# Held weight sums and a new order of the seven products in a two-layer hybrid decoder trunk

## The chip, the cores and the metric

One core of one Trainium2 chip runs the whole program. The metric is the device time of one execution in microseconds (us). The core has a matrix engine (PE, TensorE), three engines for elementwise work (DVE, ACT for ScalarE, POOL for GpSimd), a queue of transfers that SP issues and another that POOL issues, whose transfers can add to what stands at their destination.

## The reference

A trunk of two layers on 1024 tokens of width 1024, in float32. Layer 0 mixes tokens with a causal convolution module, layer 1 with a causal mean over several windows; behind each comes a SwiGLU feed-forward block of width 2816; one RMSNorm ends the trunk.

```python
for i in range(DEPTH):
    sh_m, sc_m, g_m, sh_f, sc_f, g_f = jnp.split(c_act @ ada_w[i] + ada_b[i], 6, axis=-1)
    h = modulate(rms_norm(x, norm_mix_g[i]), sh_m, sc_m)
    y = conformer_conv(h, ...) if i % 2 == 0 else multiscale_pool(h, ...)
    x = x + (1.0 + g_m)[:, None, :] * y
    h = modulate(rms_norm(x, norm_ffn_g[i]), sh_f, sc_f)
    y = (silu(h @ w_gate) * (h @ w_up)) @ w_down
    x = x + (1.0 + g_f)[:, None, :] * y
return rms_norm(x, final_g)
```

What the change touches is the last `@ w_down` of layer 1, its addition to x, and the last `rms_norm`.

## The kernel before

The activations lie with channels on the 128 partitions and tokens along the free axis; the tokens are two chunks of 512, A and B, and x is eight tiles of 128 x 512 per chunk. Float32 products are made of three matmuls each: an operand is split into a rounded high part (ScalarE's copy) and a low part (DVE's subtraction), and high x high, high x low and low x high are added up in a bank. A matmul has 512 columns, or 256 in the last piece. A loaded weight block is split the same way into a tile `w` (line 126 issues every operation of DVE, ScalarE and POOL, line 148 every matmul, lines 158 and 165 transfers of SP's and POOL's queue).

Layer 1 uses fewer products than a plain multiplication: its gate and up products come as "joints", and its down product as seven products of a 2 x 2 block scheme (Winograd's form of Strassen's). The down weights are four blocks A11, A12, A21, A22 per group q (`wds[q, 0..3]`, q = 0 to 5; a group is 128 x 1024, the last one half of it). The other side is two kinds of sums of the activations over both chunks, which the joints write to DRAM (`kinds_d`, `kept_d`; `paired` at 1237 to 1250 makes them) and which are loaded again as operands. The weights of the products are A12 (p2), A11 (p1), S2 = S1 - A11 (p6), S3 = A22 - S2 (p7), A22 (p4), S1 = A21 + A22 (p5) and S4 = A12 - S2 (p3).

`weights_of` (1426 to 1458) loads the weights of a group and splits them, `operand` (1460 to 1476) does so for the other side. For S1 and S2, SP loads one block and POOL's queue adds the other into the same tile (1438, 1440). A11 goes into a held block `s2` in a slot of the tag h0; later DVE turns it into S2, and at p3 into S4. Other blocks take one of five raw tiles. The halves of the operands take slots of h1. h0 and h1 have eight slots each, a tile waits for the last reader of the slot, and products read h0 and h1 up to the end of the joints. Per group these are eight transfers: A11, two for S1, two for S2, one each for S3, S4 and A22.

`Seven` (1482 to 1532) runs the products: a step is one group of one product, its loads are issued four steps ahead (`LOADED`) and its splits two steps ahead (`SPLIT`). A full step is 24 matmuls: two operand tiles, four banks, three each. The banks come from a pool of six; when a product is done, DVE adds the four banks to the tiles of x they belong to (`update`), which frees them. The order before:

- p2 for q 4 and 5 (its first four groups run earlier, by `one_half`), p1, p6, p7, p4, p5, then p3 for q 0, 1, 5 in p5's banks, and last p3 for q 2, 3, 4 by halves of 256 columns (`ending`).
- `final(A)`, the last norm of chunk A, begins after p4: squares, their sum over the partitions by TensorE (`var`), a root by a short chain on DVE (`col`, `var`), a spread of it over the partitions (`rstd`), then DVE multiplies each of eight tiles and SP writes it out.
- `ending` does the same for B by halves of 256 tokens, so that the first half (B1) is multiplied while the second (B2) is still summed.

The order of TensorE's work is the order of the code. A scheduler orders the other engines and the transfers by its own estimates; `order(...)` gives an instruction an edge "behind the products", so that it isn't put ahead of what TensorE does at that point of the code. In `weights_of` only POOL's adds have this edge; SP's loads haven't.

Of the kernel before, what the change touches and what calls it, by code (L numbers as in the profile page):

```python
# [16 lines left out]
P = 128  # L17
# [114 lines left out]
def trunk(ctx, tc, xT, c, vec, ada, adan, w1f, w1, wdg, w2, wgu, wdn, wds, wpl, out):  # L132
# [1043 lines left out]
    def joint(l, fp, between=None):  # L1176
        c = {}

        def part(name, banks, after, again, before=None):
            def emit(take):  # L1180
                if before is not None:
                    before()
                if not again:
                    c[banks] = two_banks(banks)
                wt, h = take(), st["T"][name]
                todo = [(o, j) for o in range(2) for j in range(4)]
                if fp == 0 and name != "n4":
                    todo.sort(key=lambda oj: oj[1])
                for o, j in todo:
                    b = c[banks][o]  # L1190
                    products(b, wt, 4 * o + j, h[j], j == 0 and not again, j == 3, more=True)
                    if j == 3:
                        after(o, b)
                        pace()
            return emit

        def load():
            c["r1"] = [tmp.tile([P, TMPW], F32, tag=tag, name=nm("r1"), bufs=2) for tag in ("acc", "ny")]
            for o, r in enumerate(c["r1"]):
                sync.dma_start(r, rd[l][fp][:, o])  # L1200

        def after6(o, b):
            c["r2", o] = r = window(512, "r2")
            V_.tensor_tensor(r, c["r1"][o], b, op=SUB)

        def after5(o, b):
            if fp:
                r = temp(512)
            else:
                c["r15"] = c["r15"] if o else block("u0", "r15", F32)  # L1210
                r = c["r15"][:, o]
            c["r15", o] = r
            V_.tensor_tensor(r, b, c["r1"][o], op=ADD)
            if STRASSEN[l] and o:
                st["taken"] = V_.last.ins.name

        def ended(r, i, f, op):
            def after(o, b):
                t = c["r1"][o] if r == "r1" else c[r, o]
                V_.tensor_tensor(t, b, t, op=op)  # L1220
                c["c", o] = t
                if fp == 0 and r == "r15" and o:
                    st["read"] = V_.last.ins.name
                    for ins in st["next"]:
                        tc.add_manual_dep(ins, st["read"], edge, reason="behind the first unit's reads")
                if o and STRASSEN[l]:
                    paired(i, f, c["c", 0], t)
                elif o:
                    gated(l, i, f, c["c", 0], t)
            return after  # L1230

        def paired(i, f, g, u):

            duo, k = kinds_d[l][fp // 2], c.setdefault("k", {})
            if i:
                if not k:
                    k[0] = block("u0", "k", F32)
                else:
                    k[1], k[2] = block("u0", "k", F32), block("u0", "k", F32)
                    sync.dma_start(k[2][:, 1], kept_d[l][fp // 2][:, fp % 2])  # L1240
                gated(l, i, f, g, u, into=k[0][:, 1 - f % 2])
                if 1 in k:
                    V_.tensor_tensor(k[1][:, 0], k[0][:, 1], k[0][:, 0], op=SUB)
            else:
                gated(l, i, f, g, u, into=k[2][:, 0])
                V_.tensor_tensor(k[1][:, 1], k[1][:, 0], k[2][:, 0], op=ADD)
                V_.tensor_tensor(k[2][:, 1], k[2][:, 1], k[1][:, 1], op=SUB)
                V_.tensor_tensor(k[0][:, 0], k[0][:, 1], k[1][:, 1], op=SUB)
# [174 lines left out]
        tag, bufs = ("raw", RAW_BUFS) if turn[0] % (RAW_BUFS + ADA_BUFS) < RAW_BUFS else ("ada", ADA_BUFS)  # L1423
        return raws.tile([P, D], F32, tag=tag, name=nm("raw"), bufs=bufs)

    def weights_of(l, kind, q):

        n = duo_width(q) * 512
        src = lambda b: wds[q, b][:, :n]
        got = {}  # L1430

        def load():
            if kind == "a11":
                r = st["s2", q] = block("h0", "s", F32).rearrange("p a b -> p (a b)")[:, :n]
            else:
                r = raw_tile()[:, :n]
            first, *plus = {"a11": (0,), "a12": (1,), "a22": (3,), "s1": (2, 3), "s2": (2, 3), "s3": (3,), "s4": (1,)}[kind]
            nc.sync.dma_start(r, src(first))
            for b in plus:
                order(nc.gpsimd.dma_start(r, src(b), accum_op=ADD))  # L1440
                clock["G"] = max(clock["G"], clock["PE"]) + 0.9
            got["raw"] = r

        def halves():
            r = got["raw"]
            if kind in ("s2", "s3", "s4"):
                h = st["s2", q]
                to = r if kind == "s3" else h
                V_.tensor_tensor(to, r, h, op=SUB)
                r = to  # L1450
            wt = wts.tile([P, 2, D], F32R, tag="w", name=nm("w"))
            S_.copy(wt[:, 0, :n], r)
            V_.tensor_tensor(wt[:, 1, :n], r, wt[:, 0, :n].bitcast(F32), op=SUB)
            return wt

        return load, halves

    def operand(l, kind, q):
# [21 lines left out]
    class Seven:  # L1480
# [23 lines left out]

        def run(self, after={}, ending=None):
            for i, (name, key, fresh, ends, qs, q) in enumerate(self.steps):
                def emit(take, i=i, key=key, fresh=fresh, ends=ends, qs=qs, q=q):
                    self.load(i + LOADED + 1)
                    self.split(i + SPLIT + 1)
                    if key is None:  # L1510
                        return
                    if fresh and q == qs[0]:
                        self.banks[key] = [bank("dn") for _ in range(4)]
                    bs, (wt, ops) = self.banks[key], self.ready.pop(i)
                    for ds in ((0, 1), (2, 3)):
                        for j, g in enumerate(ops):
                            for d in ds:
                                last = q == qs[-1] and j == len(ops) - 1
                                products(bs[d], wt, 4 * j + d, g, fresh and q == qs[0] and j == 0, last, more=True)
                                if last:  # L1520
                                    for ch, half in ends:
                                        update(ch, 4 * half + d, bs[d], gate_f, self.l)
                            pace()
                unit(emit)
                if (name, q) in after:
                    after[name, q]()
# [10 lines left out]
    def one_half(l, qs):  # L1537
# [13 lines left out]
            return emit  # L1551
        bs = []
        for q in qs:
            unit(emit_of(q, bs), lambda q=q: queued(weights_of(l, "a12", q)))

    def ending(ch, l):

# [70 lines left out]
        return upper, emit  # L1628

    def final(ch):  # L1630
        acc = yield from sum_sq(x[ch.i], ch.n)
        rstd = yield from mean_rsqrt(acc, ch.n, True, loose=True)
# [271 lines left out]
    def pool_end(ch):  # L1904
# [30 lines left out]
    upper, last_part = ending(B, 1)  # L1935
    seven.run({
        ("p1", 0): lambda: unit(lambda take: x_in(B)),
        ("p4", NQ - 1): lambda: put("final_a", lambda: final(A)),
        ("p5", NQ - 1): lambda: unit(upper),
    }, last_part)  # L1940
    run_units(W_BUFS, early)

# [60 lines left out]
```

## Time and profile before

| what | us |
|---|---|
| median of three runs | 1716.39 (1716.17 to 1717.21) |
| the profiled execution | 1717.94 |
| its span in the trace | 1716.1 |
| TensorE busy | 1676.0 (98%) |
| DVE, ScalarE, POOL busy | 1321.6, 795.3, 475.7 |

A window row gives a stretch of the span, its length, for each engine the busy time and the count of instructions, then the granted share of TensorE's clock, the busy share of the 16 DMA engines, and GB/s. A timeline or chain row gives start, duration, engine, line, what is written and read, and in brackets how long the engine stood idle before it and for whom. Times are us from the span's start. The joints of layer 1 run up to 1500, the seven products from 1500 to 1704, the end from there.

### The profile page before, as it was taken

Reading aid. Unit: us, or ns where it says so; the run is one execution under the profiler, and the core shown is the slowest. Engines: PE = TensorE matmul, PEld = TensorE weight load, DVE = VectorE, ACT = ScalarE, POOL = GpSimd, SP = SyncE. Lnnn points to the kernel's source line nnn. Section 1 sums busy time; section 2 is a strip of 40 time slices with the busy share of each in tenths; the row PEclk is TensorE's granted clock in tenths of the full one; section 3 lists DMA queues with packets and bytes.
Section 4 is the critical chain, followed back from the end, with each engine's and each line's share of the span. In section 5 each row is a group of like instructions: output and inputs, shape, how many; then the busy total and the mean of one; then the engine's idle time right before and its main releaser. Section 6 shows DMA issues by size and latency. Waiting matters only on the chain.

```text
span 1716.1 us, 21376 instructions
## 1 busy us (share of the span) xinstructions
PE 1676.0 (98%) x7614; PEld 1362.7 (79%) x7614; DVE 1321.6 (77%) x1879; ACT 795.3 (46%) x1077; POOL 475.7 (28%) x561
## 2 busy tenths in 40 slices
PE   7999999999999999999999999999999999999987
PEld 5777777778887888888888888888788888878877
DVE  8889898898669797877665987868676767685485
ACT  3678686866546233233223437637222222233433
POOL 2588767795001121221110301101111111000101
PEclk9999999999999999999999999999999999999999
DMA  8958997737775888976876748868877777675851
GB/s 303 284 169 238 232 226 200 214 98 215 245 233 135 269 288 262 301 250 240 337 266 224 258 147 240 250 222 222 224 210 221 222 224 216 236 242 171 241 179 53
DMA packets 117613, 386.48 MB, mean 225 GB/s; under 512 B 12481, under 2 KB 14657, under 8 KB 117506
## 3 DMA queue, kind: packets, MB, share of 16 engines
q1 hardware_dynamic: 79680, 253.23, 42.1%
q0 software_dynamic: 36736, 130.83, 31.1%
q8 instruction: 60, 0.98, 0.2%
q10 hardware_dynamic: 1090, 1.05, 0.2%
q14 instruction: 47, 0.39, 0.1%
HBM read 317.69 MB, written 63.18 MB: 222 GB/s over the span
## 4 chain that ended last, share of the span: by engine, by line
PE 83%; DVE 5%; DMA 5%; issue 3%; POOL 1%; ACT 1%; DVEq 0%; POOLq 0%; ACTq 0%
PE dn L148 23%; PE a L148 22%; PE e L148 13%; PE p L148 9%; PE y L148 6%; PE g L148 3%; PE first L148 3%; PE tap L148 2%; DMA raw<-in_wds_dram 2%; DMA rd<-r 1%; POOL pa L126 1%; PE ada L148 1%; DMA s<-in_wds_dram 1%; DMA adaw<-in_adan_dram 1%; DVE t L126 1%
## 5 line engine op out<-in xcount | busy, mean ns | idle before, releaser
L126 ACT CAST w<-raw 128x1024 fp32r<-128x1024 f32 (+1 forms) x249 | 259.0, 1042 | 337.8 <-PE dn L148 97.7
L148 PE MATMUL dn<-g,w 128*128 128x512 f32 x1152 | 265.2, 391 | 1.7 <-DVE g L126 1.0
L126 DVE TENSOR_TENSOR w<-raw,w 128x1024 fp32r<-128x1024 f32 x177 | 217.9, 1234 | 52.7 <-ACT w L126 52.5
L148 PEld LDWEIGHTS dn<-g,w 128*128 128x128 f32 x1152 | 215.7, 188 | 47.6 <-DVE g L126 1.3
L148 PE MATMUL a<-n,w 128*128 128x512 f32 x1056 | 248.0, 390 | 1.2 <-DVE n L126 0.7
L148 PE MATMUL p<-h,w 128*128 128x512 f32 x1056 | 244.5, 391 | 1.7 <-ACT r L126 1.1
L126 POOL TENSOR_TENSOR pa<-pa,pr 128x512 f32<-128x512 f32 x160 | 227.6, 1507 | 23.4 <-ACT pr L126 17.1
L148 PEld LDWEIGHTS a<-n,w 128*128 128x128 f32 x1056 | 197.8, 188 | 44.6 <-DVE n L126 2.2
L148 PEld LDWEIGHTS p<-h,w 128*128 128x128 f32 x1056 | 197.2, 188 | 45.0 <-ACT r L126 2.3
L148 PE MATMUL dn<-hi,w 128*128 128x512 f32 (+1 forms) x600 | 177.4, 378 | 5.3 <-DVE x L126 5.3
L126 DVE SCALAR_TENSOR_TENSOR ca<-u,vecs,ca 128x512 f32<-128x512 f32 x245 | 169.7, 745 | 0.5
L126 DVE SCALAR_TENSOR_TENSOR x<-dn,gains,x 128x512 f32<-128x512 f32 (+1 forms) x140 | 98.4, 730 | 48.6 <-PE dn L148 48.6
L148 PEld LDWEIGHTS dn<-hi,w 128*128 128x128 f32 x600 | 111.0, 191 | 28.3 <-DVE x L126 7.2
L148 PE MATMUL a<-t,w 128*128 128x512 f32 x528 | 126.1, 395 | 4.6 <-DVE w L126 2.9
L148 PE MATMUL e<-b,w 128*128 128x512 f32 x528 | 123.4, 390 | 0.6 <-DVE r L126 0.6
L148 PE MATMUL e<-t,w 128*128 128x512 f32 x528 | 123.3, 389 | 0.0
L148 PEld LDWEIGHTS a<-t,w 128*128 128x128 f32 x528 | 100.5, 191 | 26.8 <-DVE w L126 3.8
L126 ACT ACTIVATE pr<-u,vecs 128x512 f32<-128x512 f32 x160 | 108.2, 716 | 24.3 <-POOL pa L126 18.8
L148 PEld LDWEIGHTS e<-b,w 128*128 128x128 f32 x528 | 99.1, 188 | 21.6 <-DVE r L126 1.0
L148 PEld LDWEIGHTS e<-t,w 128*128 128x128 f32 x528 | 99.1, 188 | 20.5
L1108 POOL DMA_DIRECT2D raw<-in_wgu_dram x41 | 36.3, 885 | 281.7 <-DVE k L126 88.3
L148 PE MATMUL dn<-lo,w 128*128 128x512 f32 (+1 forms) x300 | 112.9, 376 | 0.0
(179 smaller groups left out, 2371.3 us busy)
## 6 DMA issues: line engine op xcount, KB each, us to landing
raw<-in_wgu_dram SPq DMA_DIRECT2D x132, 512.0 KB, 5.1
adaw<-in_ada_dram POOLq DMA_DIRECT2D x48, 512.0 KB, 7.2
raw<-in_wdn_dram SPq DMA_DIRECT2D x44, 512.0 KB, 8.4
raw<-in_wgu_dram POOLq DMA_DIRECT2D x41, 512.0 KB, 7.1
raw<-in_w_dram SPq DMA_DIRECT2D x36, 512.0 KB, 6.3
gd<-g POOLq DMA_DIRECT2D x36, 512.0 KB, 7.8
g<-gd SPq DMA_DIRECT2D x36, 512.0 KB, 5.7
kinds<-k POOLq DMA_DIRECT2D x33, 512.0 KB, 7.2
```

The costliest lines, as they stand in the source:

```text
L126: self.last = self.order(getattr(self.eng, name)(out, *args, **kw))
L148: last_mm[0] = nc.tensor.matmul(out, lhsT, rhs, start=start, stop=stop, skip_group_check=more).ins.name
L1108: d = order(nc.gpsimd.dma_start(w[i], wgu[l, fp, src], accum_op=ADD))
```

## The change

Weights: the held block becomes a sum `sum`, now in h1, while the operand halves move to h0. It is A11 at first; after the split of S1 for p5, DVE subtracts S1 from it, which makes it -S2, the weights of p6 as they stand (`paired` writes p6's operand negated instead); p7 takes A22 as loaded plus the sum; and at p3 POOL's queue adds A12 into it, which makes S4. Per group these are six transfers instead of eight. All loads and adds of `weights_of` but those of `one_half` now have the edge "behind the products".

Order: p2, p1, p5, p6, p7, p4, p3. p5 is second of the full ones; two of its banks are the two spare ones (tag `ca`), it ends with updates of both halves of B, and p3 begins with banks of its own. The split for the step after next stands behind the products at a product's last group. The four loads of x's chunk B stand behind p1's groups 0 to 3, one each.

The last norm of A: it begins after p7 with four squares, the other four wait for the end of p4; ScalarE multiplies by `final_g`, then POOL multiplies five tiles and DVE three by the root, and a transfer takes two tiles.

```diff
-    def weights_of(l, kind, q):
+    def weights_of(l, kind, q, placed=True):
...
+        def behind_products(d):
+            if placed and last_mm[0] is not None:
+                tc.add_manual_dep(d.ins, last_mm[0], edge, reason="behind the products")
...
             if kind == "a11":
-                r = st["s2", q] = block("h0", "s", F32).rearrange("p a b -> p (a b)")[:, :n]
+                st["sum", q] = block("h1", "s", F32).rearrange("p a b -> p (a b)")[:, :n]
+            if kind in ("a11", "s2", "s4"):
+                r = st["sum", q]
             else:
-                r = raw_tile()[:, :n]
-            first, *plus = {"a11": (0,), "a12": (1,), "a22": (3,), "s1": (2, 3), "s2": (2, 3), "s3": (3,), "s4": (1,)}[kind]
-            nc.sync.dma_start(r, src(first))
-            for b in plus:
-                order(nc.gpsimd.dma_start(r, src(b), accum_op=ADD))
+                r = (raw_tile() if placed else raws.tile([P, D], F32, tag="raw", name=nm("raw")))[:, :n]
+            first = {"a11": 0, "a12": 1, "a22": 3, "s1": 2, "s3": 3}.get(kind)
+            if first is not None:
+                behind_products(nc.sync.dma_start(r, src(first)))
+            if kind in ("s1", "s4"):
+                plus(r, src(3 if kind == "s1" else 1))
...
-            if kind in ("s2", "s3", "s4"):
-                h = st["s2", q]
-                to = r if kind == "s3" else h
-                V_.tensor_tensor(to, r, h, op=SUB)
-                r = to
+            if kind == "s3":
+                V_.tensor_tensor(r, r, st["sum", q], op=ADD)
...
+            if kind == "s1":
+                V_.tensor_tensor(st["sum", q], st["sum", q], r, op=SUB)
...
-            hi, lo = block("h1", "hi"), block("h1", "lo")
+            hi, lo = block("h0", "hi"), block("h0", "lo")
...
-                        self.banks[key] = [bank("dn") for _ in range(4)]
+                        self.banks[key] = [spare_bank("dn") if name == "p5" and d > 1 else bank("dn") for d in range(4)]
...
+        for k in range(KT):
+            S_.activation(x[ch.i][k], x[ch.i][k], AF.Copy, scale=V("final_g", k))
+        rstd = yield from steps
         for k in range(KT):
             xs = x[ch.i][k]
-            V_.scalar_tensor_tensor(xs, xs, V("final_g", k), rstd, op0=MUL, op1=MUL)
-            nc.sync.dma_start(out[:, k, ch.t0 : ch.t0 + ch.n], xs)
+            (V_ if k % 3 == 1 else G_).tensor_tensor(xs, xs, rstd, op=MUL)
+            if k % 2:
+                nc.sync.dma_start(out[:, k - 1 : k + 1, ch.t0 : ch.t0 + ch.n], xp[ch.i][k // 2])
...
         ("p1", "a11", "b11", "x", True, [(A, 0)], every),
+        ("p5", "s1", "t1", "y", True, [(B, 1), (B, 0)], every),
...
-        ("p5", "s1", "t1", "y", True, [(B, 1)], every),
-        ("p3", "s4", "b22", "y", False, [(B, 0)], short),
+        ("p3", "s4", "b22", "y", True, [(B, 0)], short),
```

What this moves is seen at three places. The first is POOL's queue in layer 1's first joint: `in_wds` are the down weights, `w` a sum of gate and up weights, `kept` an operand written to DRAM, `n` an operand of the joint. Before:

```order
L488 DMA w_9751<-in_wgu_dram 128x1024
L1440 DMA raw_12285<-in_wds_dram 128x1024
L1096 DMA w_9852<-raw_9842 128x1024
L1440 DMA raw_12321<-in_wds_dram 128x1024
L165 DMA kept_4_203<-t_9880 128x512
L1440 DMA raw_12357<-in_wds_dram 128x1024
L165 DMA kept_4_203<-t_9947 128x512
L1096 DMA w_9919<-raw_9844 128x1024
L1333 DMA n_1596_10043<-af_9586 128x512
L1333 DMA n_1597_10048<-af_9589 128x512
L1333 DMA n_1598_10053<-af_9613 128x512
```

And now:

```order
L488 DMA w_9751<-in_wgu_dram 128x1024
L1096 DMA w_9852<-raw_9842 128x1024
L165 DMA kept_4_203<-t_9880 128x512
L165 DMA kept_4_203<-t_9947 128x512
L1096 DMA w_9919<-raw_9844 128x1024
L1333 DMA n_1596_10043<-af_9586 128x512
L1333 DMA n_1597_10048<-af_9589 128x512
L1333 DMA n_1598_10053<-af_9613 128x512
L1333 DMA n_1599_10058<-af_9698 128x512
```

The three adds into raw tiles of the down weights (line 1440) are gone from here; they stand near the end of POOL's row now. SP's five loads of the same blocks leave this place too.

The second is DVE where p2 passes to p1: `k` are sums that go to DRAM, `w` and `lo` low halves, `s` the held block, `x_10797` x's first two tiles with `dn` the banks of p2. Before:

```order
L126 TENSOR_TENSOR k_12095<-k_12095,k_12096 128x512
L126 TENSOR_TENSOR w_12141<-s_12017,w_12141 128x1024
L126 TENSOR_TENSOR k_12096<-k_12096,k_12095 128x512
L126 TENSOR_TENSOR k_12065<-k_12065,k_12095 128x512
L126 TENSOR_TENSOR w_12180<-s_12021,w_12180 128x1024
L126 TENSOR_TENSOR s_12017<-raw_12285,s_12017 128x1024
L126 TENSOR_TENSOR w_12207<-s_12137,w_12207 128x1024
L126 TENSOR_TENSOR s_12021<-raw_12321,s_12021 128x1024
L126 SCALAR_TENSOR_TENSOR x_10797<-dn_12148,gains,x_10797 128x512
```

And now:

```order
L126 TENSOR_TENSOR w_12196<-s_12021,w_12196 128x1024
L126 TENSOR_TENSOR k_12095<-k_12065 128x512
L126 TENSOR_TENSOR r_1860_11945<-a_11949,r_1860_11945 128x512
L126 TENSOR_TENSOR lo_12145<-op_12019,hi_12144 128x1024
L126 TENSOR_TENSOR r_1861_11946<-a_11950,r_1861_11946 128x512
L126 TENSOR_TENSOR lo_12200<-op_12023,hi_12199 128x1024
L126 TENSOR_TENSOR k_12096<-r_1861_11946,t_12128 128x512
L126 TENSOR_TENSOR w_12207<-s_12137,w_12207 128x1024
L126 SCALAR_TENSOR_TENSOR k_12095<-k_12095,k_12096 128x512
L126 TENSOR_TENSOR k_12096<-k_12096,k_12095 128x512
L126 TENSOR_TENSOR k_12065<-k_12065,k_12095 128x512
L126 SCALAR_TENSOR_TENSOR x_10797<-dn_12148,gains,x_10797 128x512
```

Ahead of the first update of x, the two subtractions into `s` are gone, and of the three low halves of A11 (`w<-s`) one is left directly ahead of it, one stands among the k and r of the joint, and the first further ahead.

The third is POOL's last work, the multiplications by the root `ny`: 128x512 is chunk A, 128x256 a half of B. Before:

```order
L126 TENSOR_TENSOR x_12242<-x_12242,ny_13635 128x256
L126 TENSOR_TENSOR x_12244<-x_12244,ny_13635 128x256 x2
L126 TENSOR_TENSOR x_12246<-x_12246,ny_13635 128x256
L126 TENSOR_TENSOR x_12248<-x_12248,ny_13635 128x256 x2
L126 TENSOR_TENSOR x_12244<-x_12244,ny_13676 128x256
L126 TENSOR_TENSOR x_12248<-x_12248,ny_13676 128x256
```

And now:

```order
L126 TENSOR_TENSOR x_10989<-x_10989,ny_13578 128x512 x2
L126 TENSOR_TENSOR x_11373<-x_11373,ny_13578 128x512
L126 TENSOR_TENSOR x_11181<-x_11181,ny_13578 128x512
L126 TENSOR_TENSOR x_10797<-x_10797,ny_13578 128x512
L126 TENSOR_TENSOR x_12242<-x_12242,ny_13617 128x256
L126 TENSOR_TENSOR x_12279<-x_12279,ny_13617 128x256 x2
L126 TENSOR_TENSOR x_12317<-x_12317,ny_13617 128x256
L126 TENSOR_TENSOR x_12355<-x_12355,ny_13617 128x256 x2
L126 TENSOR_TENSOR x_12279<-x_12279,ny_13658 128x256
L126 TENSOR_TENSOR x_12355<-x_12355,ny_13658 128x256
```

Five multiplications of chunk A stand ahead of the same eight of chunk B.

More of the change, by code (lines that the diff above doesn't have):

```diff
@@ L1245, in paired @@
                 gated(l, i, f, g, u, into=k[2][:, 0])
-                V_.tensor_tensor(k[1][:, 1], k[1][:, 0], k[2][:, 0], op=ADD)
-                V_.tensor_tensor(k[2][:, 1], k[2][:, 1], k[1][:, 1], op=SUB)
-                V_.tensor_tensor(k[0][:, 0], k[0][:, 1], k[1][:, 1], op=SUB)
+                V_.scalar_tensor_tensor(k[1][:, 1], k[1][:, 0], -1.0, k[2][:, 0], op0=MUL, op1=SUB)
+                V_.tensor_tensor(k[2][:, 1], k[2][:, 1], k[1][:, 1], op=ADD)
+                V_.tensor_tensor(k[0][:, 0], k[0][:, 1], k[1][:, 1], op=ADD)
                 for b in (2, 1, 0):
@@ L1430, in weights_of, with plus @@
         got = {}
+        def behind_products(d):
+            if placed and last_mm[0] is not None:
+                tc.add_manual_dep(d.ins, last_mm[0], edge, reason="behind the products")
+        def plus(r, what):
+            behind_products(nc.gpsimd.dma_start(r, what, accum_op=ADD))
+            clock["G"] = max(clock["G"], clock["PE"]) + 0.9
         def load():
             if kind == "a11":
-                r = st["s2", q] = block("h0", "s", F32).rearrange("p a b -> p (a b)")[:, :n]
-            else:
-                r = raw_tile()[:, :n]
-            first, *plus = {"a11": (0,), "a12": (1,), "a22": (3,), "s1": (2, 3), "s2": (2, 3), "s3": (3,), "s4": (1,)}[kind]
-            nc.sync.dma_start(r, src(first))
-            for b in plus:
-                order(nc.gpsimd.dma_start(r, src(b), accum_op=ADD))
-                clock["G"] = max(clock["G"], clock["PE"]) + 0.9
+                st["sum", q] = block("h1", "s", F32).rearrange("p a b -> p (a b)")[:, :n]
+            if kind in ("a11", "s2", "s4"):
+                r = st["sum", q]
+            else:
+                r = (raw_tile() if placed else raws.tile([P, D], F32, tag="raw", name=nm("raw")))[:, :n]
[4 more added lines that the diff above has]
+                plus(r, src(3 if kind == "s1" else 1))
             got["raw"] = r
@@ L1506, in run, with emit @@
             for i, (name, key, fresh, ends, qs, q) in enumerate(self.steps):
-                def emit(take, i=i, key=key, fresh=fresh, ends=ends, qs=qs, q=q):
+                def emit(take, i=i, name=name, key=key, fresh=fresh, ends=ends, qs=qs, q=q):
                     self.load(i + LOADED + 1)
-                    self.split(i + SPLIT + 1)
+                    if key is None or q != qs[-1]:
+                        self.split(i + SPLIT + 1)
                     if key is None:
@@ L1523, in emit @@
                             pace()
+                    self.split(i + SPLIT + 1)
                 unit(emit)
@@ L1553, in one_half @@
         for q in qs:
-            unit(emit_of(q, bs), lambda q=q: queued(weights_of(l, "a12", q)))
+            unit(emit_of(q, bs), lambda q=q: queued(weights_of(l, "a12", q, False)))
     def ending(ch, l):
@@ L1630, in final @@
     def final(ch):
-        acc = yield from sum_sq(x[ch.i], ch.n)
-        rstd = yield from mean_rsqrt(acc, ch.n, True, loose=True)
+        acc = temp(ch.n, "acc", 2)
+        for k in range(KT):
+            while k == KT // 2 and "a_done" not in st:
+                yield "wait"
+            sq = temp(ch.n) if k else acc
+            S_.activation(sq, x[ch.i][k], AF.Square)
+            if k == KT - 1:
+                V_.scalar_tensor_tensor(acc, sq, EPS_SUM, acc, op0=ADD, op1=ADD)
+            elif k:
+                V_.tensor_tensor(acc, acc, sq, op=ADD)
+            yield
+        steps = mean_rsqrt(acc, ch.n, True, loose=True)
+        yield next(steps)
+        for k in range(KT):
+            S_.activation(x[ch.i][k], x[ch.i][k], AF.Copy, scale=V("final_g", k))
+        rstd = yield from steps
         for k in range(KT):
             xs = x[ch.i][k]
-            V_.scalar_tensor_tensor(xs, xs, V("final_g", k), rstd, op0=MUL, op1=MUL)
-            nc.sync.dma_start(out[:, k, ch.t0 : ch.t0 + ch.n], xs)
+            (V_ if k % 3 == 1 else G_).tensor_tensor(xs, xs, rstd, op=MUL)
+            if k % 2:
+                nc.sync.dma_start(out[:, k - 1 : k + 1, ch.t0 : ch.t0 + ch.n], xp[ch.i][k // 2])
             yield
@@ L1935, in trunk, with final_begins @@
     upper, last_part = ending(B, 1)
+    def final_begins():
+        put("final_a", lambda: final(A))
+        unit(upper)
     seven.run({
-        ("p1", 0): lambda: unit(lambda take: x_in(B)),
-        ("p4", NQ - 1): lambda: put("final_a", lambda: final(A)),
-        ("p5", NQ - 1): lambda: unit(upper),
+        **{("p1", m): lambda m=m: unit(lambda take: x_in(B, m)) for m in range(KT // 2)},
+        ("p7", NQ - 1): final_begins,
+        ("p4", NQ - 1): lambda: unit(lambda take: st.__setitem__("a_done", True)),
     }, last_part)
```

## The prediction

> **What bounds the kernel now.** I read the page first, for the bounding engine, then the windows, to find where that engine is not full, then the waits and the chain at those places, last the groups of the end.
>
> ```profile
> span 1716.1 us, 21376 instructions
> PE 1676.0 (98%) x7614; PEld 1362.7 (79%) x7614; DVE 1321.6 (77%) x1879; ACT 795.3 (46%) x1077; POOL 475.7 (28%) x561
> PE 83%; DVE 5%; DMA 5%; issue 3%; POOL 1%; ACT 1%; DVEq 0%; POOLq 0%; ACTq 0%
> ```
>
> TensorE is busy for 98% of the span and carries 83% of the chain. The program issues the same matmuls after the change as before, so the change can only win time that TensorE stands still, runs at a lower granted clock, or has finished. The windows (columns: stretch, length, busy time and count of each engine, granted clock, DMA share, GB/s) show what is there to win.
>
> ```profile
> 1400.00:1500.00 100.00, 100.00 (x443) 82.86 (x442) 67.71 (x86) 27.39 (x32) 10.22 (x15) 1.00 0.70 223
> 1220.00:1230.00 10.00, 6.05 (x19) 4.29 (x18) 8.81 (x11) 5.45 (x6) 0.00 (x0) 0.72 0.44 111
> 1510.00:1520.00 10.00, 6.79 (x23) 4.68 (x22) 10.00 (x12) 4.85 (x6) 0.88 (x1) 0.83 0.84 271
> 1630.00:1640.00 10.00, 8.55 (x38) 6.79 (x37) 7.85 (x9) 5.15 (x6) 0.02 (x1) 1.00 0.71 201
> 1650.00:1660.00 10.00, 7.69 (x34) 6.08 (x33) 8.30 (x17) 2.00 (x2) 0.00 (x0) 0.90 0.45 159
> ```
>
> A full stretch holds 443 matmuls in 100 us, 0.2257 us each. The other rows are holes: one where layer 1's first joint passes to the second (1220 to 1234), and three inside the down stage of seven products, at the seams between them. Two more places are not in these rows: a short wait at 1131, and the end, after the last product.
>
> **The change part by part: transfers that no longer come early.** Before, the five earliest weight groups of the down stage are loaded long ahead, and three of them get an accumulating transfer on POOL's queue in the middle of the first joint. The chain over that place (start, duration, what) and TensorE there:
>
> ```profile
> 1192.30 5.80 DMA raw<-in_wds_dram
> 1198.86 0.66 POOL raw L1440
> 1201.22 3.23 issue
> 1209.81 0.85 POOL n L1333
> 1210.93 10.23 DMA raw<-in_wgu_dram
> ...
> 1197.44 0.64 ACT L126 ACTIVATE n<-af 128x512 fp32r<-128x512 f32 x1
> ...
> 1209.98 11.89 PE L148 MATMUL a<-n,w 128*128 128x512 f32 x48
> 1223.59 0.73 PE L148 MATMUL a<-t,w 128*128 128x512 f32 x2 [1.73 <-ACT w L126]
> 1226.54 7.46 PE L148 MATMUL a<-t,w 128*128 128x512 f32 x22 [2.22 <-DVE w L126]
> ```
>
> From 1209.98 to 1234.00 TensorE does 72 matmuls, worth 72 x 0.2257 = 16.3 us, in 24.0: 7.7 us are lost. The cause is POOL's queue, which is worked off in order: the add at 1198.86 waited for a load issued at 1192.30, and behind it stand a weight add, four adds for n (the last at 1209.81) and then the load at 1210.93 that DVE waits for. These adds land slowly once they are queued:
>
> ```profile
> n<-af POOLq DMA_DIRECT2D x4, 256.0 KB, 8.3
> ```
>
> After the change the three adds and five loads stand far behind, next to the down stage. ScalarE has written what the n adds read by 1198.1 (1197.44 + 0.64), so they can leave about then; the load that landed at 1221.16 lands some 8 to 10 us earlier, well ahead of TensorE's first wait. I take -7.0 of the 7.7; the rest stays for the load's new neighbours. Bounds: -7.7 if nothing is left; -3.9 if half of the queue's delay is that of the weight add and the n adds themselves, which stay.
>
> The hole at 1131 is the same thing in small: ScalarE waits for such a load ahead of the copy that frees a bank.
>
> ```profile
> 1115.51 8.77 DMA raw<-in_wds_dram
> 1131.86 5.74 PE L148 MATMUL p<-h,w 128*128 128x512 f32 x24 [0.87 <-ACT r L126]
> ```
>
> In the new order the two loads of this kind (SP's queue) come ahead of two loads for other weights instead of behind them. That is worth the idle time, -0.9, between 0 (another late load takes the place) and -1.1.
>
> **p2 to p1.** The second half of p1's four banks comes from p2, whose results DVE must first add to x. DVE is late for it:
>
> ```profile
> 1493.12 6.45 SPq L1438 DMA_DIRECT2D s<-in_wds_dram  x6
> 1505.41 1.05 ACT L126 CAST w<-s 128x1024 fp32r<-128x1024 f32 x1 [6.11 <-DMA s<-in_wds_dram]
> 1509.98 1.22 DVE L126 TENSOR_TENSOR s<-raw,s 128x1024 f32<-128x1024 f32 x1
> 1513.38 0.75 DVE L126 SCALAR_TENSOR_TENSOR x<-dn,gains,x 128x512 f32<-128x512 f32 x1
> 1514.18 0.50 PE L148 MATMUL dn<-hi,w 128*128 128x512 f32 x1 [2.74 <-DVE x L126]
> 1515.98 0.79 PE L148 MATMUL dn<-hi,w 128*128 128x512 f32 x1 [0.47 <-DVE x L126]
> ```
>
> The window 1510 to 1520 has 23 matmuls, 5.2 us of work, so 4.8 are lost: 3.2 of waiting, the rest at a granted clock of 0.83. The six loads of A11 (s) leave one by one from 1493 to 1499, as the joint's last products release h0; ScalarE waits 6.1 us for the first, and everything that DVE does with them, the two subtractions into S2 among it (1.22 each, the one at 1509.98 and its like), is queued ahead of the updates of x. After the change A11 goes to h1, which is free by then, the two subtractions are gone from here, and two of the three splits of A11 stand earlier in DVE's row. Without the subtractions the update at 1513.38 comes 2 x 1.22 earlier, at 1510.9, and with one split out of the way at 1509.7; with its 0.75 it is done at 1510.5, and TensorE wants the bank at about 1511.1. What has to wait for h0 now are p2's and p1's operand halves; the first of them finds a slot at 1493, seven us ahead of p2. I take -4.8; bounds -3 (these halves delay p2's start at 1500 by 2) and -5.5.
>
> **p4 to p5, the wait of final(A), p5 to p3.** These are pieces of the chain:
>
> ```profile
> 1632.97 3.47 DMA raw<-in_wds_dram
> 1639.01 7.79 PE dn L148 x33
> 1655.89 1.05 PE var L148 x8
> 1656.95 7.21 PE dn L148 x24
> 1672.51 26.85 PE dn L148 x168
> ...
> PE var L148 <- DVE acc L126: 2.3, 1, 2.3
> PE dn L148 <- DVE x L126: 5.3, 4, 2.7
> ```
>
> TensorE waits 5.3 us for x in four places, of which 3.2 were counted; 2.1 are left, 1.45 ahead of 1639.01 and 0.6 ahead of 1672.51. The 33 matmuls behind the first take 7.79 instead of 7.45, +0.3. The sum of squares comes 2.3 late at 1655.89, and the 24 matmuls behind it take 7.21 instead of 5.42, +1.8. Together 6.5. In the new order the end of p4 no longer meets a DVE that waits for a load, as it did for S4 until 1636.4 (1632.97 + 3.47); the squares of A start early and its var stands 36 half products into p3, well behind them; p3 takes fresh banks. So -6.5. One new wait comes in at p6 to p7: DVE's addition of raw A22 and the sum, which waits for A22's load, stands between the first and the second update of x there; behind it in DVE's queue is that second update, and p7's second bank waits for it. I take one 1.2-us addition less what the bank order covers, 0.95, and 0.35 of lower clock behind it as behind 1639.01: +1.3, between 0 and +2.8 if the load is late by another 1.5. The four more updates of p5 (0.75 each) lie beside 5.4 us of matmuls per group and cost nothing.
>
> That slow matmuls follow a gap is in the rows (2.3 us idle, then 0.90 granted). The Trainium skill, "TensorE: Matmul & The Clock Gate", Part 1, says that the clock halves only after an idle window of about 3.4 us. By that rule the gaps of this stage would cost their idle time alone, and the slow clock behind them, 1.6 + 0.3 + 1.8 = 3.7 us of this sum, would not be there to win, which makes 1706.2; the trace does not bear the threshold out as a length of a single gap.
>
> **The end.** T is the end of the last product.
>
> ```profile
> 1699.70 4.41 PE dn L148 x36
> 1705.04 5.65 POOL L126 TENSOR_TENSOR x<-x,ny 128x256 f32<-128x256 f32 x8 [75.03 <-ACT ny L126]
> 1709.24 2.08 DVE L126 TENSOR_TENSOR x<-x,rstd 128x256 f32<-128x256 f32 x6 [1.27 <-ACT ny L126]
> L126 POOL TENSOR_TENSOR u<-u,ny 128x512 f32<-128x512 f32 x3 | 3.5, 1401 | 0.0
> L126 DVE SCALAR_TENSOR_TENSOR x<-x,vecs,ny 128x512 f32<-128x512 f32 x8 | 5.4, 748 | 0.2 <-ACT ny L126 0.2
> ```
>
> Before, T is 1704.1; the last multiplication ends at 1711.3 and the span 4.8 later (the last transfers out): 12.0 us of end. A's own eight multiplications (0.75 each) were done on DVE long before. After, A's rstd stands 18 half products (18 x 0.12 = 2.2 us) before T in TensorE's order, so ScalarE's copy of it is ready near T-1.45. POOL then has five multiplications for A (5 x 1.40 = 7.0, to T+5.55) ahead of its eight for B (8 x 0.71 = 5.7): T+11.2. DVE's three for A (2.2 us) stand in the midst of B's short chain, whose last multiplication moves from T+7.2 to about T+9.4. With 4.8 behind: T+16.0, so +4.0. Bounds: +1 if A's rstd comes earlier by enough to hide four of the five, +7 if A's last 512-KB transfers also meet B's. The Trainium skill, "GPSIMD Engine Reference", section 3.1, makes DVE the engine for elementwise work and gives 1.96 times DVE's time for an addition of two tensors; the rows' 1401 against 748 ns agree, and by that rule this part of the change is a loss.
>
> **Sum.** -0.9 - 7.0 - 4.8 - 6.5 + 1.3 + 4.0 = -13.9. The profiled execution took 1717.94 (its span 1716.1 and 1.84 around it), 1.55 more than the median of 1716.39 of the three runs shown. 1716.39 - 13.9 = 1702.5.
>
> **The rivals.** (1) The joint's hole does not close: something else than the three adds holds POOL's queue, for instance the weight add and the n adds themselves. For it: the chain has 3.23 us of "issue" at 1201.22, a wait for which it shows no releaser. Against it: the adds for n leave slowly only behind the add of 1198.86, though what they read was written by 1198.1. Time: 1702.5 + 7.0 = 1709.5. Chance 0.15.
>
> (2) The other sign: p5 put second starves. Its weights need a load and then an add into the same tile, one behind the other.
>
> ```profile
> raw<-in_wds_dram SPq DMA_DIRECT2D x20, 512.0 KB, 4.8
> raw<-in_wds_dram POOLq DMA_DIRECT2D x5, 512.0 KB, 9.1
> ```
>
> A group is 24 matmuls, 5.42 us. Four groups are loaded ahead, 21.7 us, against 4.8 + 9.1 + 2.3 (copy and subtraction) = 16.2: enough, as long as POOL's adds overlap. Should each add leave only when the one before it has landed, a group takes 9.1 instead of 5.42 and p5's 5.5 groups lose 20 us: 1722.7, slower. It decides from the point where a group takes more than 5.42 + 17.3/5.5 = 8.6 us. For it: load, add and operand are 1.57 MB a group, 290 GB/s in 5.42 us, with the loads of x beside them, and the window 1510 to 1520 moved 271. Against it: the load at 1210.93 left POOL 1.1 us behind the add at 1209.81, although those adds take 8.3 us to land, so several are under way at once. Chance 0.08.
>
> (3) The end is as long as before, or shorter by luck of the order, with the stage as forecast: 1702.5 - 4 = 1698.5. Chance 0.12. That the change would not take away what it says is ruled out by counting: SP's loads of these blocks go from 42 to 30 in the new order, POOL's adds stay 12.
>
> The forecast itself has 0.65: its bounds, added in part, give 1698 to 1708.
>
> **The numbers.** Predicted 1702.5. The range takes in rivals 1 and 3 and stops short of rival 2: 1696 to 1711. No change, within 0.2% (3.4 us, about what a measurement of this kernel can tell), is 1713 to 1719.8: the upper part of rival 1 with a long end, and a p5 that starves a little, 0.04; slower 0.08; faster 0.88.
>
> **What would show it.** Right: no wait of TensorE between 1205 and 1240; the four adds for n issued before 1203; no x wait over 1 us at p2 to p1; one wait of about a microsecond at p6 to p7; POOL's last multiplication about 11 us behind the last product, with five of 1.4 us ahead of it. Wrong: TensorE waiting for w inside p5 at every group (rival 2), an unchanged wait near 1224 (rival 1), or a new hole where the loads went, between 1500 and 1530.

## The result and the profile after

| | us |
|---|---|
| before, median of 4 runs | 1716.80 (1716.17 to 1718.06) |
| changed, median of 4 runs | 1707.93 (1706.91 to 1708.65) |
| ratio | 0.9947, 95% interval 0.993 to 0.9964 |
| the changed kernel's profiled execution, its span | 1708.65, 1706.9 |

The change gains 8.9 us by the medians; forecast were 13.9 and a time of 1702.5, with a range of 1696 to 1711. Two profiled executions, cut at the first and the last product of the down stage, show where the 9.2 us between their spans came from. The cuts are the first and last row `dn` of TensorE; the last product ends at its start plus its duration (before 1704.11, after 1688.80 + 0.28 = 1689.08).

| | before | after | difference | forecast |
|---|---|---|---|---|
| up to the stage's first product | 1500.4 | 1492.6 | -7.8 | -7.9 |
| the stage, first to last product | 203.7 | 196.5 | -7.2 | -10.0 |
| the end, behind the last product | 12.0 | 17.8 | +5.8 | +4.0 |

The page after, the rows that answer to those of before:

```profile
span 1706.9 us, 21328 instructions
PE 1671.0 (98%) x7614; PEld 1361.9 (80%) x7614; DVE 1318.9 (77%) x1872; ACT 799.5 (47%) x1085; POOL 483.1 (28%) x566
PE 86%; DVE 6%; DMA 3%; ACT 1%; issue 1%; POOL 1%; SPq 0%; DVEq 0%; ACTq 0%
```

Transfers fell from 5% to 3% of the chain, DVE rose from 5% to 6%. The windows over the old holes and the new ones (columns as before: stretch, length, each engine, granted clock, DMA share, GB/s):

```profile
1210.00:1220.00 10.00, 9.89 (x44) 7.89 (x43) 5.93 (x9) 3.97 (x6) 0.00 (x0) 1.00 0.28 83
1220.00:1230.00 10.00, 10.00 (x46) 8.24 (x45) 8.96 (x11) 2.19 (x3) 0.56 (x1) 1.00 0.67 226
1500.00:1510.00 10.00, 10.00 (x46) 8.29 (x45) 8.28 (x9) 4.64 (x5) 0.22 (x1) 1.00 0.70 254
1540.00:1550.00 10.00, 8.52 (x38) 6.71 (x37) 9.62 (x9) 4.37 (x5) 1.74 (x2) 1.00 0.98 252
1590.00:1600.00 10.00, 8.41 (x37) 6.64 (x37) 10.00 (x11) 4.17 (x5) 0.00 (x0) 1.00 0.42 142
1620.00:1630.00 10.00, 8.73 (x37) 6.62 (x37) 9.61 (x12) 9.73 (x16) 0.00 (x0) 1.00 0.59 194
1690.00:1700.00 10.00, 4.77 (x20) 4.42 (x20) 4.99 (x18) 1.67 (x4) 9.40 (x11) 0.62 0.71 262
```

The joint's hole near 1223 is closed, 46 matmuls in 10 us. So is that of p2 to p1, which lies in the window 1500 to 1510 now, since the stage starts sooner. Three new ones stand in the stage, and the end has grown. In POOL's queue the four adds for n now leave from 1193.74 to 1197.80, where they left from 1201.13 to 1209.81; the profile shows the first and the last of them released by ScalarE, which wrote what they read. The load behind them leaves at 1200.95 instead of 1210.93:

```profile
1191.27 0.89 POOL L1096 DMA_DIRECT2D w<-raw  x1 [1.02 <-PE p L148]
1193.74 0.88 POOL L1333 DMA_DIRECT2D n<-af  x1 [1.58 <-ACT n L126]
1197.80 0.88 POOL L1333 DMA_DIRECT2D n<-af  x1 [0.83 <-ACT n L126]
1200.95 0.87 POOL L1108 DMA_DIRECT2D raw<-in_wgu_dram  x1 [2.27 <-issue]
```

All waits of TensorE from the first product to the end, from its timeline, with the first and the last product themselves:

```profile
1492.59 0.39 PE L148 MATMUL dn<-hi,w 128*128 128x512 f32 x1
1543.64 0.74 PE L148 MATMUL dn<-hi,w 128*128 128x512 f32 x2 [1.48 <-DVE w L126]
1594.76 0.50 PE L148 MATMUL dn<-hi,w 128*128 128x512 f32 x1 [1.59 <-DVE x L126]
1624.79 0.47 PE L148 MATMUL dn<-hi,w 128*128 128x512 f32 x1 [0.50 <-ACT w L126]
1626.49 0.50 PE L148 MATMUL dn<-hi,w 128*128 128x512 f32 x1 [0.77 <-DVE x L126]
1688.80 0.28 PE L148 MATMUL dn<-hi,w 128*128 128x256 f32 x1
1692.70 1.23 PE L148 MATMUL rstd<-ident,col 128*128 128x128 f32 x4 [3.62 <-DVE col L126]
1698.30 1.19 PE L148 MATMUL rstd<-ident,col 128*128 128x128 f32 x4 [2.02 <-DVE col L126]
```

The first is inside p5, the second at p6 to p7, the next two at p7 to p4. The transfers behind them stand in the chain, the first of them an add on POOL's queue for p5, the others loads of A22:

```profile
1530.71 9.36 DMA raw<-in_wds_dram
1581.61 8.25 DMA raw<-in_wds_dram
1607.02 13.15 DMA raw<-in_wds_dram
```

The last two waits above are in the end, where DVE and POOL multiply A while B's roots are made:

```profile
1687.59 0.69 DVE L126 TENSOR_TENSOR x<-x,ny 128x512 f32<-128x512 f32 x1
1687.64 11.74 POOL L126 TENSOR_TENSOR x<-x,ny 128x512 f32<-128x512 f32 x11 [81.01 <-ACT ny L126]
1688.20 1.25 DVE L126 SCALAR_TENSOR_TENSOR var<-col 128x2 f32<-128x2 f32 x1
1689.37 2.35 DVE L126 TENSOR_TENSOR x<-x,ny 128x512 f32<-128x512 f32 x2
1699.93 2.07 DVE L126 TENSOR_TENSOR x<-x,rstd 128x256 f32<-128x256 f32 x6 [1.78 <-ACT ny L126]
1699.98 1.41 POOL L126 TENSOR_TENSOR x<-x,ny 128x256 f32<-128x256 f32 x2 [0.60 <-ACT ny L126]
```

B1's root waits behind A's multiplications on DVE and is spread 3.6 us after the last product; in the kernel before, it was spread 0.2 ahead of the last product's end (1704.11):

```profile
1703.95 0.60 PE L148 MATMUL rstd<-ident,col 128*128 128x128 f32 x4
```

DVE's last work ends at 1702.0, 12.9 us behind the last product, where it was 7.2. POOL's last work ends at 1701.4, after POOL had stood idle for 0.6 us until B2's root was there.

### The profile page after: what moved, and what is told of

Its sections match the earlier page's. It is cut to its first block, busy times and chain, and to the rows that moved or that the text cites. A ratio compares the mean times of both kernels' runs of the same rounds, so it can differ in the third digit from the quotient of the medians.

```text
span 1706.9 us, 21328 instructions
## 1 busy us (share of the span) xinstructions
PE 1671.0 (98%) x7614; PEld 1361.9 (80%) x7614; DVE 1318.9 (77%) x1872; ACT 799.5 (47%) x1085; POOL 483.1 (28%) x566
## 4 chain that ended last, share of the span: by engine, by line
PE 86%; DVE 6%; DMA 3%; ACT 1%; issue 1%; POOL 1%; SPq 0%; DVEq 0%; ACTq 0%
PE a L148 23%; PE dn L148 21%; PE e L148 13%; PE p L148 12%; PE y L148 6%; PE g L148 3%; PE first L148 3%; PE tap L148 2%; DMA raw<-in_wds_dram 2%; POOL pa L126 1%; PE ada L148 1%; DVE t L126 1%; DMA adaw<-in_adan_dram 1%; DMA op<-kinds 1%; DVE x L126 1%
## 5 line engine op out<-in xcount | busy, mean ns | idle before, releaser
L148 PEld LDWEIGHTS a<-t,w 128*128 128x128 f32 x528 | 99.0, 188 | 21.6 <-DVE w L126 1.1
```

The lines of the kernel that those rows point to most:

```text
L148: last_mm[0] = nc.tensor.matmul(out, lhsT, rhs, start=start, stop=stop, skip_group_check=more).ins.name
```

## The experiments

Theory: the joint's gain comes from three adds that leave POOL's queue there; the stage's gain from fewer transfers and the new order, less what loads that are no longer early cost; the loss at the end from A's root, which comes so late that A's multiplications fall into B's. The rivals stand with each run. This table holds what the profiles gave (first product, stage, end, span, us) and the timed ratio to the kernel before with its interval. Kernels with the same program up to 1490 differ there by up to 3.5 us from one execution to another (1491.5 to 1495.0), so a start is read no finer than that in this table. Nearly all of this difference arises ahead of 1102. A transfer of POOL's queue there, ahead of the places at 1131 and 1223, gives a closer measure (before, changed, and changed without edges, in this order):

```profile
1101.30 0.86 POOL L488 DMA_DIRECT2D w<-in_wgu_dram  x1 [4.31 <-PE p L148]
1101.78 0.86 POOL L488 DMA_DIRECT2D w<-in_wgu_dram  x1 [4.93 <-PE p L148]
1104.12 0.86 POOL L488 DMA_DIRECT2D w<-in_wgu_dram  x1 [4.48 <-PE p L148]
```

From this transfer to the stage's first product it is 399.1 us in the kernel before, 390.8 in all eight profiles of the changed kernel and its variants that keep the edge on the adds, and 399.6 in the changed kernel without edges. In the kernel before with the edges it is 391.9 (loads and adds) and 392.9 (adds alone).

| kernel | first product | stage | end | span | ratio |
|---|---|---|---|---|---|
| before | 1500.4 | 203.7 | 12.0 | 1716.1 | 1 |
| before, edges on loads and adds | 1493.5 | 207.2 | 11.8 | 1712.6 | 0.9991 (0.9978 to 1.0004) |
| before, edges on adds alone | 1494.7 | 202.1 | 12.8 | 1709.5 | 0.9949 (0.9935 to 0.9962) |
| changed | 1492.6 | 196.5 | 17.8 | 1706.9 | 0.9947 (0.993 to 0.9964) |
| changed, again | 1493.7 | 196.4 | 17.4 | 1707.5 | 0.9928 (0.9914 to 0.9943) |
| changed, no edges | 1503.7 | 191.4 | 17.7 | 1712.8 | 0.9962 (0.9948 to 0.9976) |
| changed, x loaded at p5 | 1492.2 | 196.4 | 17.4 | 1706.0 | 0.9941 (0.9927 to 0.9956) |
| changed, A multiplied on DVE | 1493.7 | 195.4 | 17.5 | 1706.5 | 0.993 (0.9917 to 0.9944) |
| changed, A's root sooner | 1491.5 | 194.3 | 11.7 | 1697.5 | 0.9901 (0.9886 to 0.9917) |
| the same, again | 1495.0 | 193.8 | 11.7 | 1700.6 | 0.991 (0.9895 to 0.9926) |
| root sooner, five steps ahead | 1492.3 | 196.0 | 12.2 | 1700.6 | 0.9909 (0.9895 to 0.9922) |
| root sooner, edges on adds alone | 1492.0 | 191.4 | 12.5 | 1695.9 | 0.9874 (0.9856 to 0.9891) |

In the kernel before, POOL's adds go through `order`, but that gives its edge only where a switch is set (`behind[0]`, line 152), and it isn't set while a step of the seven products issues its loads. So the three adds in the joint had no edge, and the edges below are new for adds and loads alike.

**The edges alone, in the kernel before.**

```diff
...
-            nc.sync.dma_start(r, src(first))
+            behind_products(nc.sync.dma_start(r, src(first)))
             for b in plus:
-                order(nc.gpsimd.dma_start(r, src(b), accum_op=ADD))
+                behind_products(nc.gpsimd.dma_start(r, src(b), accum_op=ADD))
...
```

> The kernel before, with one part of the change: all loads and adds of the seven products' weights but p2's early ones get the edge behind the products, so five loads and three adds leave layer 1's first joint; order, held block and transfers stay. My theory (POOL's queue was held up by these adds): TensorE's waits at 1131 and 1223 to 1226 go, the first product of the stage starts 7 to 8 us earlier than the 1500.4 of before, and the whole run is 5 to 8 us shorter, near 1710. Rival (the weight add and the n adds hold the queue themselves): the waits near 1223 stay above 2 us and the time stays within 2 us of 1716.5. The stage itself may gain or lose a few us, since its own loads come later now.

Measured: no wait near 1223, the stage 6.9 us sooner. The wait at 1131 did not go, against the expectation. The stage is 3.5 longer, with six waits for x in it, and the time is not clearly below that of before:

```profile
1132.05 5.76 PE L148 MATMUL p<-h,w 128*128 128x512 f32 x24 [0.71 <-ACT r L126]
1493.53 0.39 PE L148 MATMUL dn<-hi,w 128*128 128x512 f32 x1
```

The list of TensorE's waits inside the stage (us in total, times, longest):

```profile
PE dn L148 <- DVE x L126: 9.8, 6, 3.2
```

So the edges close the joint's hole, and half of it comes back in the stage, whose loads now come when the stage runs. The forecast of 5 to 8 us for the whole run was wrong; the part of it that left room for a loss in the stage held.

**The adds alone, in the kernel before.** The same edge on the `accum_op=ADD` transfers only; the five loads of SP stay in the joint.

> The kernel before, with the edge on POOL's adds alone: three adds leave layer 1's first joint, the five loads on SP's queue stay in it. My theory (the adds in POOL's queue are what holds the n adds up): the wait near 1223 falls below 1 us and the stage's first product starts at 1494 or earlier instead of 1500.4. Rival (the loads crowd the transfers): the wait stays at 3 us or more in all, the first product at 1498 or later.

```profile
1494.67 0.39 PE L148 MATMUL dn<-hi,w 128*128 128x512 f32 x1
1537.19 0.76 PE L148 MATMUL dn<-hi,w 128*128 128x512 f32 x1 [4.28 <-DVE x L126]
```

There is no wait near 1223 with the loads still there, so the adds are the cause and the rival falls. The wait at 1131 is there, with 1.75 us. The stage gets a wait of 4.3 us at p1 to p6 and loses others. The ratio, 0.9949, is as good as that of the whole change.

**The change without its edges.**

```diff
         def behind_products(d):
-            if placed and last_mm[0] is not None:
-                tc.add_manual_dep(d.ins, last_mm[0], edge, reason="behind the products")
+            if False:
+                pass
```

> The changed kernel without the edges behind the products, so that five loads and three adds of the down weights come back into layer 1's first joint; fewer transfers, p5 second and the new last norm stay. My theory (the joint's gain of 7 to 8 us comes from the edges alone): TensorE waits again near 1223 for about 4 us, the stage's first product moves back to 1499 to 1501, the stage itself is as short as before or 1 to 2 us shorter, since its first loads are early, and the run takes 5 to 8 us more than the changed kernel. Rival (two transfers fewer and the new order take the hole away too): the first product stays at 1493 and the time within 2 us of the changed kernel's.

```profile
1219.84 0.50 PE L148 MATMUL a<-n,w 128*128 128x512 f32 x1 [0.63 <-DMA n<-af]
1222.18 3.51 PE L148 MATMUL a<-n,w 128*128 128x512 f32 x14 [1.38 <-DMA n<-af]
1227.50 0.73 PE L148 MATMUL a<-t,w 128*128 128x512 f32 x2 [1.81 <-ACT w L126]
1230.45 6.87 PE L148 MATMUL a<-t,w 128*128 128x512 f32 x22 [2.22 <-DVE w L126]
1503.72 0.39 PE L148 MATMUL dn<-hi,w 128*128 128x512 f32 x1
```

The joint's hole is back, 6.0 us of waiting, this time also for the n adds themselves. The first product comes 11 us later than in the changed kernel; 2.3 of them are there already at the transfer of 1104.12, so the edges are worth 8.8, a little more than expected. There is no wait at 1131. And the stage is 191.4 us and has no wait of TensorE at all. The new order and six transfers a group are thus worth 203.7 - 191.4 = 12.3 us in the stage, and the edges take 5.1 of them back.

**x's loads later.** `("p1", m)` becomes `("p5", m)` for the four loads of x's chunk B.

> The changed kernel, with the four loads of x's chunk B behind p5's first groups instead of p1's. If these loads starve p5's weights (my theory for the wait of 1.48 us in p5's third group, where a load of an operand took 11.3 us and an add 9.4), that wait goes or falls below 0.5 us and the run is 1 to 2 us shorter, near 1706.3. Rival (POOL's adds are slow by themselves, or are issued late because DVE and ScalarE are behind): the wait stays at 1 us or more and the time within 0.7 us of 1707.9.

```profile
1548.74 0.72 PE L148 MATMUL dn<-hi,w 128*128 128x512 f32 x2 [1.53 <-DVE w L126]
```

The wait moved by one group and kept its size, and the time did not change, so the theory's forecast was wrong. The run does not clear x's loads, though: they were issued from 1535 to 1553 here, beside the late add for p5 (issued at 1536.53, 9.8 us). In the second profile of the changed kernel, with x's loads where they were, and in both with A's root sooner, the wait inside p5 is absent, so it is there in some executions only.

**A multiplied on DVE.** All eight multiplications by the root on `V_`.

> The changed kernel, with all eight multiplications of chunk A's last norm on DVE and none on POOL. In the changed kernel three of them took 0.69, 1.2 and 1.2 us on DVE while POOL multiplied, and an operation on 128x2 took 1.25 instead of 0.17. If POOL's work slows DVE's (my theory), the eight take 0.6 to 0.7 each here, about 5 us, B's short chain loses some 3 us by standing behind them, POOL is free for B 7 us sooner, and the end is 15 to 17 us: 1705 to 1707. If DVE is slow there for a reason of its own, they take about 1.2 each, 9 to 10 us, and the run is 3 us or more longer than 1708.

```profile
1688.21 3.69 DVE L126 TENSOR_TENSOR x<-x,ny 128x512 f32<-128x512 f32 x6
1692.89 1.22 PE L148 MATMUL rstd<-ident,col 128*128 128x128 f32 x4 [3.87 <-DVE col L126]
1694.61 4.14 POOL L126 TENSOR_TENSOR x<-x,ny 128x256 f32<-128x256 f32 x6 [88.36 <-ACT ny L126]
```

With POOL idle the six in a row take 0.62 us each, so POOL's work is what slowed DVE. But the end is 17.5 us, above the 15 to 17 expected: B1's root waits 3.87 us instead of 3.62, now behind seven quick multiplications (the eighth comes after it) instead of three slow ones. The ratio of 0.993 is as near to the changed kernel's second (0.9928) as that is to its first (0.9947): no difference is resolved.

**A's root sooner.**

```diff
-        steps = mean_rsqrt(acc, ch.n, True, loose=True)
+        steps = mean_rsqrt(acc, ch.n, True, when="soon", loose=True)
```

> The changed kernel, with the sum over the partitions in chunk A's last norm put into TensorE's order sooner (about 8 us), so that A's root is spread some 13 us before the last product instead of 2.9. My theory (the end is 5.8 us longer because A's multiplications on POOL and DVE fall into B's): the five on POOL are over before B's begin, the end from the last product to the end of the span goes from 17.8 back to 12 to 14 us, and the run takes 1702 to 1704. Rival (the end is longer because of A's larger output transfers, or because the two tiles' transfers meet): the end stays above 16 us and the time near 1707.

```profile
1673.10 4.10 DVE L126 TENSOR_TENSOR x<-x,ny 128x512 f32<-128x512 f32 x3
1673.15 8.07 POOL L126 TENSOR_TENSOR x<-x,ny 128x512 f32<-128x512 f32 x5 [70.14 <-ACT ny L126]
1685.54 0.28 PE L148 MATMUL dn<-hi,w 128*128 128x256 f32 x1
1686.75 5.66 POOL L126 TENSOR_TENSOR x<-x,ny 128x256 f32<-128x256 f32 x8 [5.52 <-ACT ny L126]
```

A's multiplications are over 4.6 us ahead of the last product, POOL waits 5.5 us for B, and the end is 11.7 us. All of the loss at the end was the place of A's root in TensorE's order. The control beside the last run agrees:

> The run with A's root sooner once more, as the control of the one beside it. Both theories: 0.989 to 0.991 of the kernel before, an end of 11.5 to 12.5 us, waits of 1 to 3 us in all at the seams of the seven products.

It had 0.991 and the same end, with three waits of 2.0 us in all in the stage.

**Loads five steps ahead.** `LOADED = 5`, on top of the sooner root; and the changed kernel again beside it.

> The changed kernel with A's root sooner (as in the run on that) and loads five steps ahead instead of four. My theory (the waits at p6 to p7 and p7 to p4, 1.05 and 1.39 us there, are DVE waiting for a load of A22 issued one step too late): both fall below 0.5 us and the run is 1 to 3 us shorter than with four steps, 1699 to 1701. Rival (the transfers are at their limit and more loads ahead only crowd others): no shorter, or a wait elsewhere.

> The changed kernel itself again, beside the next three on one chip. Both theories: 0.993 to 0.996 of the kernel before; the profile has the waits of the first one, and the single wait inside p5 (1.48 us before) may be there or not.

```profile
1593.18 0.77 PE L148 MATMUL dn<-hi,w 128*128 128x512 f32 x1 [2.77 <-DVE x L126]
```

The waits at p7 to p4 went, the one at p6 to p7 grew to 2.77, and the ratio is that of four steps. The forecast of 1 to 3 us was wrong: a step more does not help, as the rival had it.

**The best of it.** The sooner root, with the edge on POOL's adds alone.

> The changed kernel with A's root sooner, and with the edge behind the products on POOL's adds alone, so that SP's loads of the down weights go early again. My theory (the adds alone make the joint's hole; early loads alone make the stage short, as in the run without edges, 191.2 us from first to last product): no wait above 1 us near 1223, first product at 1491 to 1495, stage 191 to 193 us, end 12 us, 1695 to 1699 in all. Rival (the stage was short there because its adds came early too): the stage stays at 194 to 196 us and the time within 1 us of the run with A's root sooner.

```profile
1491.97 0.39 PE L148 MATMUL dn<-hi,w 128*128 128x512 f32 x1
1684.62 0.38 PE L148 MATMUL var<-ones,t 128*128 128x1 f32 x2 [0.44 <-ACT t L126]
```

TensorE does not wait once from 1200 to the last product; the first wait after the joint is that of 0.44 in the end. The stage starts as soon as in the changed kernel, so it is not a late start that makes it short. The stage is 191.4 us as without edges, the joint has no hole, the end is 12.5. The median is 1697.63, the ratio 0.9874: 21.6 us below the kernel before and some 10 below the changed one. It adds up from parts shown one by one.

## Why the prediction was right, and where it was not

**The joint** (-7.0): right in cause and size. Counted from the transfer at 1101 the first product came 8.3 us sooner, where 7.9 were forecast with the hole at 1131, the waits are gone, and the run with the edge on the adds alone shows that it is the adds and not the loads. Rival 1 is out: once they were gone, the weight add and the n adds did not hold each other up. The load behind them still stood for 2.27 us as "issue".

**1131** (-0.9): the wait is gone, and for the reason that the prediction gave here, not for the joint's. With the edges alone it stayed (0.71 and 1.75 us); in the changed kernel it is gone with and without edges. SP issued the two loads of this kind at 1115.51 and 1126.69 before, and at 1101.38 and 1106.82 now, ahead of the two loads of other weights.

**p2 to p1** (-4.8): right, TensorE has no wait there and 46 matmuls in the window 1500 to 1510, where the seam lies now. The edges alone would not have done it: in the kernel before they take the wait away from p2 to p1, but one of 3.85 us in all (3.21 and 0.64), or of 4.28 with the adds alone, stands at p1 to p6 in its place. The changed kernel without edges has neither, so it is the held sum and the new order that remove it; no run parts these two.

**p4 to p5, the wait of final(A), p5 to p3** (-6.5): those three waits are gone as forecast.

**The new waits** (+1.3): this is the step that was too small. "One new wait comes in at p6 to p7" was right in place and cause, with 1.59 and 2.57 us (0.67 + 1.90) of waiting in the two profiles where 0.95 was taken and 2.45 was the bound (2.8 with 0.35 of lower clock), but it is not the only one: p7 to p4 cost 1.27 and 0.49, and p5 1.48 in one profile. What the prediction left out is the other side of its first part. It took the early loads as a burden and priced their going at a gain alone; but loads that were early are work that the stage need not do. The kernels with and without edges measure it: 203.7 to 207.2 before the change, 191.4 to 196.5 with it. It is SP's loads: with the edge on the adds alone the stage is 202.1 and 191.4. Had the stage been as short as it could be with early loads, the forecast of -10.0 would have been too small instead.

**The end** (+4.0, measured +5.8): that A's root is late and that five multiplications of A stand ahead of B's on POOL was right, and POOL began 1.4 us ahead of the last product's end, as forecast. The path was wrong. The prediction let POOL end last, at T+11.2, and B's short chain on DVE with its multiplications at T+9.4; DVE ended last, at T+12.9, and POOL, at T+12.3, had waited for the same chain. The price was off there: this chain was to lose 2.2 us and lost 5.7. DVE's multiplications of A took 0.69 + 2.35 instead of 2.2, a small operation 1.25 instead of 0.17, and TensorE, all but idle, spread the root in 1.23 us where the same four matmuls had taken 0.60.

The Trainium skill's "GPSIMD Engine Reference", section 3.1, would have POOL be the wrong engine for it. The run with all of it on DVE shows that this is not what cost the time: its end was 17.5.

All in all the time lies at the upper edge of the 1698 to 1708 that the bounds gave: what the change takes away was forecast well, and what it brings in was priced too low twice.

**Rival 2**, p5 starved for good and the run slower, did not come: p5 lost 1.5 us in one of the changed kernel's two profiles. It was right that its weights are just in time.

## What to carry to other kernels

A transfer that is issued early has two sides: the queue that it stands in may hold up something more urgent, and the stage that it serves finds it done; price both, per queue, before moving it. Here only the accumulating adds on POOL's queue were in the way, and the plain loads of SP's queue belonged early. When the order of products changes, follow the last step of each chunk to the end as well: a root put some 11 us too late in TensorE's order cost 5.8 us.

## What the runs showed of the hardware

A transfer on POOL's queue seems to be held by transfers well ahead of it. In the kernel before, POOL issued three of the n adds at 1204.47, 1207.90 and 1209.81 and the load behind them at 1210.93; each time a transfer issued three or four places earlier had landed 0.31 us before (at 1204.16, 1207.59, 1209.50 and 1210.62). The first two of these were the last of the three adds of down weights and the weight add behind it. That the landing is what released them is read from these times alone. The 3.23 us of "issue" in the prediction's chain end with the first of them.

An elementwise operation of DVE on two operands slows when POOL does the same: 128x512 took 0.62 us in a row without POOL (3.69 for six) and 1.37 with it (4.10 for three), while POOL's took 1.61 (8.07 for five) instead of 1.40; one tiny DVE operation of 0.17 took 1.25. It is not so every time: the first of A's three in the changed kernel took 0.69 beside POOL. The prediction set POOL's 1401 ns against 748 of another operation of DVE; for the same multiplication POOL takes 1.40 against 0.62, 2.3 times as long.

TensorE's speed after a gap is not a matter of the gap's length alone. The Trainium skill, "TensorE: Matmul & The Clock Gate", Part 1, names an idle window of about 3.4 us. The same wait of 1.74 us for the second half's root was followed by a spread of 0.68 us in the run with A's root sooner

```profile
1689.83 0.68 PE L148 MATMUL rstd<-ident,col 128*128 128x128 f32 x4 [1.74 <-DVE col L126]
```

and of 1.19 in the best one,

```profile
1687.41 1.19 PE L148 MATMUL rstd<-ident,col 128*128 128x128 f32 x4 [1.74 <-DVE col L126]
```

a difference that a length of idle time alone does not tell. In the stage the waits of 1.48 and 1.59 us left the granted clock at 1.00 in the windows quoted above.

Why p5's wait comes in some executions and not in others stays open.
